# One core, one layer step with Mamba-2 and sparse attention: seven re-orderings in a hand-scheduled kernel (attention units in one visit, tanh of the convolution apart from its taps, a third weight buffer, bias tables by matmul, quads in the state update)

## The chip, the cores and the metric

The kernel runs on one core of one Trainium2 chip, as one launch. The metric is the device time of one execution in microseconds (us). The kernel before was timed three times: 1399.72, 1389.86 and 1389.57 us, median 1389.86. The profile is of one execution of its own, which took 1398.44 us.

## The reference

One inference step of a decoder layer for two request groups that share the weights: a prompt of 256 tokens, and 8 samples of 8 new tokens each over 2048 cached positions. Together they are 320 columns of activations.

```python
def layer_forward(x, ssm_state, conv_state, nsa_fn, bias_tab, lw):
    x = x + 0.5 * swiglu_ffn(rmsnorm(x, ffn1_norm), ffn1_w_in, ffn1_w_out)
    h = rmsnorm(x, mix_norm)
    z, xbc, dt_raw, q, kv, nsa_g, merge_g = jnp.split(h @ w_in_proj, cuts, axis=-1)
    y_ssm, new_conv, new_ssm = mamba_mixer(z, xbc, dt_raw, conv_state, ssm_state, ...)
    q = rmsnorm(q.reshape(b, L, KV_HEADS, Q_PER_KV, HEAD_DIM), qk_norm[0]) * (HEAD_DIM ** -0.5)
    ...
    gates = jax.nn.sigmoid(nsa_g.astype(f32)).reshape(b, L, KV_HEADS, Q_PER_KV, 3)
    o, new_win = nsa_fn(q, gates, paged_rows, win_rows, compress_kv, bias_tab)
    gm = jax.nn.sigmoid(merge_g.astype(f32))
    y_a = (y_ssm @ w_branch_ssm).astype(f32)
    y_b = (o.reshape(b, L, D_ATTN).astype(x.dtype) @ w_branch_attn).astype(f32)
    mix = (gm[..., :D_MODEL] * y_a + gm[..., D_MODEL:] * y_b).astype(x.dtype) @ w_out
    x = x + mix
    x = x + 0.5 * swiglu_ffn(rmsnorm(x, ffn2_norm), ffn2_w_in, ffn2_w_out)

def causal_conv(xbc, conv_state, w, b):          # in mamba_mixer, before the state update
    ...
    y = b + sum(xp[:, k:k + L] * w[k] for k in range(D_CONV))
    return jax.nn.silu(y), xp[:, L:]

def ssd(x, dt, A, Bm, Cm, h0):                   # in mamba_mixer: chunked scan
    ...
    states = jnp.einsum('bclgn,bclgjp->bcgjpn', Bc, xdt * decay_to_end[..., None])
    ...
    y_off = jnp.einsum('bclgn,bcgjpn->bclgjp', Cc, h_start) * decay_from_start[..., None]

def nsa_block(...):                              # nsa_fn, per block of queries
    ...                                          # three softmaxes with a relative bias on each score:
    return gates[..., 0:1] * o_c + gates[..., 1:2] * o_s + gates[..., 2:3] * o_w
```

The three branches of the attention are compressed keys (`o_c`), the best blocks of keys (`o_s`) and a window (`o_w`).

## The kernel before

**Dense work.** Every large product goes through `dense` (L327). Weights are split in two fp32r halves, as are the activations, so a step over 128 rows of weights (a k-step) is three matmuls of 128x128 by 320 columns: L342, L343 and L344. The kernel has 1928 k-steps, in this order: FFN1, the projection of q, k and v, that of the convolution's channels (xBC), the merge gates, z, the two branch products and `w_out`, FFN2.

**Weights.** They come in blocks of 8 k-steps (128x1024) through the queue of SP (`w_load`, L305) into one of `NRAW` = 2 raw buffers. ACT casts a block to its high half `wh` (L314), DVE subtracts to the low half `wl` (L323), and only then the next load is issued. Cast and subtraction run two blocks ahead of the matmuls.

**Order.** Each engine works through its instructions in the order in which the program issues them. That order is written by generators: after each k-step `tick` (L143) adds half of the stage's number in `RATE` (L116) to a credit, and for each whole credit one generator goes on to its next `yield`. What the generators put on PE in one such step lies between two k-steps and is called a visit here. `S.defer(n, f)` runs f after 2n k-steps. So attention, compression of the cache and the state update lie between the dense matmuls, and a wait of any of them on PE holds up everything behind it.

**The places of the change.**

- Convolution (`conv_unit`, L1199): one unit per 128 channels; 4 k-steps after its projection three taps on DVE, directly followed by the tanh on ACT; the gate on DVE 8 k-steps after the projection.
- Attention: 32 units of the prompt (xBC stage) and 40 of the samples (z stage), 8 batches of 5. A unit has a visit with the transposes of the next unit (L1302, L1457) and scores (L1431) further ahead, then a `yield`, then a visit with its own values (L1319, L1471). ACT copies transposed weights to `pT` or `sT`. At each batch edge of the samples ACT copies the sums to `R` (L1477).
- Bias tables `tb` and `cb`: each of their 128 rows is a shifted row of a reversed table that lies in DRAM (`trev`): 16 strided DMAs on SP (`load_bias`, L837). `flip`, a constant, is loaded by SP just before them (L849).
- State update of the samples (`sample_chunks`, four groups q of 8 batches): states `h` come 4 ahead (`AHEAD`) into 6 buffers (`NH`), on SP (L1726). For two batches at a time PE does two output products from the states (L1772, 32 columns of the array) and for each of them two products of the update (L1778 with 128 rows, L1779 with the low half, 64 rows). POOL decays h (L1775), DVE adds (L1780), SP stores it (L1679).

```python
                    if b % 2 == 0:
                        for x_ in range(2):
                            r = 32 * ((b + x_) % 4)
                            pe.matmul(py[r : r + 32, :], cz[:, b + x_, :], pend["h", j + x_], start=b + x_ < 4,
                                      stop=b + x_ >= 4)
                    ...
                    pe.matmul(p, bz[:, b, :], xh, start=True, stop=False)
                    pe.matmul(p, bz[:64, b, :], xl, start=False, stop=True)
                    v.tensor_tensor(h0, h0, p, op=ALU.add)
                    store("outH")
                    pend["outH"] = O["ssmS"][b, :, 512 * q : 512 * q + 512], h0
                    load_h(j + AHEAD)
```

## Time and profile before

| | |
|---|---|
| three runs, median | 1399.72, 1389.86, 1389.57 us: 1389.86 us |
| profiled execution | 1398.44 us, span of the trace 1396.4 us |
| granted TensorE clock, mean of the span | 0.961 |
| busy: PE (matmuls), PEld (weight loads) | 1329.4 us (95%), 1177.7 us (84%) |
| busy: DVE, ACT, POOL | 866.0, 592.8, 363.5 us (62%, 42%, 26%) |
| moved by DMA | 251.66 MB, 180 GB/s in the mean |

The span is the trace from the first to the last instruction; a share is busy time over it. Busy PE contains matmuls that run at half the clock, and matmuls that wait for their weights, so 95% isn't 95% of what PE can do. The granted clock is given as a share of 2.4 GHz: 1.00 is 2.4 GHz all through, 0.5 is 1.2 GHz all through, and a value between them says how the stretch divides between the two levels.

### The profile page before, as it was taken

To read this page: it belongs to the slowest core of one execution; us is meant where nothing else is said; L and a number is where in the kernel's file an instruction comes from. 1 tells how busy PE (TensorE), PEld (TensorE's weight loads), DVE (VectorE), ACT (ScalarE), POOL (GpSimd) and SP (SyncE) were. 2 spreads that over 40 slices of the span, in tenths; PEclk is the share of its full clock that TensorE was granted. 3 is DMA by queue.
4 is the path that set the end of the run, shared out by engine and by line. 5 is a ranking of instruction groups with operands and counts; after the bars stand their busy time and mean duration, and the time that the engine had idled before them with its cause. 6 is when DMAs were issued, how large, how long until landed. Compare 5 with 4: busy or idle time off the path is not lost.

```text
span 1396.4 us, 28186 instructions
## 1 busy us (share of the span) xinstructions
PE 1329.4 (95%) x10583; PEld 1177.7 (84%) x10583; DVE 866.0 (62%) x1862; ACT 592.8 (42%) x1152; POOL 363.5 (26%) x616
## 2 busy tenths in 40 slices
PE   8999999999979999889989989799999999999998
PEld 7899999999858878677877756577677999999998
DVE  5577656655556457866567657657767766666533
ACT  4454543445434324446544343255555344333322
POOL 2222212222000216554444435233340010000000
PEclk9999999999989999889999999999999999999999
DMA  7556656666544325421177686778894443444453
GB/s 258 164 192 201 221 184 198 210 205 201 209 100 126 125 96 198 182 91 61 50 197 214 190 237 181 290 249 314 267 333 148 168 140 134 149 149 151 148 171 110
DMA packets 107041, 251.66 MB, mean 180 GB/s; under 512 B 23208, under 2 KB 49849, under 8 KB 104953
## 3 DMA queue, kind: packets, MB, share of 16 engines
q1 hardware_dynamic: 89946, 198.27, 44.2%
q0 software_dynamic: 16960, 51.61, 11.1%
q8 instruction: 83, 1.36, 0.4%
q14 instruction: 52, 0.43, 0.1%
HBM read 235.11 MB, written 23.10 MB: 185 GB/s over the span
## 4 chain that ended last, share of the span: by engine, by line
PE 72%; DVE 11%; DMA 5%; issue 4%; ACT 4%; SPq 2%; POOL 1%; POOLq 0%; ACTq 0%; DVEq 0%
PE ps_pd L342 18%; PE ps_pd L343 16%; PE ps_pd L344 16%; DVE wl L323 3%; PE ps_sc L671 2%; PE ps_sc L672 2%; PE ps_sc L681 2%; ACT wh L314 2%; PE ps_sc L1431 2%; DVE cvo L1198 2%; PE ps_po L1471 1%; DMA out_ssmS<-h 1%; PE ps_pt L1457 1%; PE ps_po L1319 1%; PE ps_sc L1270 1%
## 5 line engine op out<-in xcount | busy, mean ns | idle before, releaser
L323 DVE TENSOR_TENSOR wl<-wraw,wh 128x1024 fp32r<-128x1024 f32 (+1 forms) x245 | 302.0, 1233 | 266.9 <-ACT wh L314 266.4
L342 PE MATMUL ps_pd<-hh,wh 128*128 128x320 f32 x1320 | 452.5, 343 | 4.5 <-ACT hh L751 1.8
L343 PE MATMUL ps_pd<-hl,wh 128*128 128x320 f32 x1320 | 418.0, 317 | 1.6 <-DVE hl L450 1.4
L344 PE MATMUL ps_pd<-hh,wl 128*128 128x320 f32 x1320 | 417.2, 316 | 0.0
L314 ACT CAST wh<-wraw 128x1024 fp32r<-128x1024 f32 (+1 forms) x245 | 252.7, 1031 | 167.2 <-PE ps_pd L343 125.0
L342 PEld LDWEIGHTS ps_pd<-hh,wh 128*128 128x128 f32 x1320 | 257.4, 195 | 44.6 <-issue 32.8
L343 PEld LDWEIGHTS ps_pd<-hl,wh 128*128 128x128 f32 x1320 | 257.6, 195 | 10.2 <-issue 5.3
L344 PEld LDWEIGHTS ps_pd<-hh,wl 128*128 128x128 f32 x1320 | 256.5, 194 | 0.0
L342 PE MATMUL ps_pd<-ah,wh 128*128 128x320 f32 x352 | 109.4, 311 | 0.0
L344 PE MATMUL ps_pd<-ah,wl 128*128 128x320 f32 x352 | 108.7, 309 | 0.0
L343 PE MATMUL ps_pd<-al,wh 128*128 128x320 f32 x320 | 98.7, 309 | 0.0
L563 POOL DMA_DIRECT2D pg<-in_cache x136 | 74.3, 547 | 73.6 <-DVE pgl L575 30.6
L235 POOL TENSOR_SCALAR ah<-ff 128x320 fp32r<-128x320 f32 x44 | 20.1, 458 | 277.9 <-DVE ff L478 277.8
L575 DVE TENSOR_TENSOR pgl<-pg,pgh 128x512 fp32r<-128x512 f32 x128 | 82.4, 685 | 15.1 <-ACT pgh L568 14.9
L1384 POOL DMA_DIRECT2D KV<-in_cache x102 | 55.0, 539 | 104.3 <-PE ps_po L1471 68.5
L473 ACT ACTIVATE sg<-sg 128x320 f32<-128x320 f32 x44 | 20.8, 472 | 135.1 <-DVE sg L472 135.0
L568 ACT CAST pgh<-pg 128x512 fp32r<-128x512 f32 x128 | 72.6, 616 | 9.0 <-PE ps_sc L672 7.3
L671 PE MATMUL ps_sc<-pgh,w1h 128*128 128x256 f32 x256 | 68.6, 289 | 2.5 <-ACT pgh L568 2.5
L672 PE MATMUL ps_sc<-pgh,w1l 128*128 128x256 f32 x256 | 68.6, 288 | 0.0
L342 PEld LDWEIGHTS ps_pd<-ah,wh 128*128 128x128 f32 x352 | 66.1, 188 | 0.5
L344 PEld LDWEIGHTS ps_pd<-ah,wl 128*128 128x128 f32 x352 | 66.1, 188 | 0.0
L343 PEld LDWEIGHTS ps_pd<-al,wh 128*128 128x128 f32 x320 | 60.2, 188 | 0.0
(453 smaller groups left out, 2250.2 us busy)
## 6 DMA issues: line engine op xcount, KB each, us to landing
wraw<-in_wproj SPq DMA_DIRECT2D x77, 512.0 KB
KV<-in_cache POOLq DMA_DIRECT2D x102, 256.0 KB, 5.4
wraw<-in_w1in SPq DMA_DIRECT2D x44, 512.0 KB
wraw<-in_w2in SPq DMA_DIRECT2D x44, 512.0 KB
pg<-in_cache POOLq DMA_DIRECT2D x136, 128.0 KB, 4.1
pg<-in_cache SPq DMA_DIRECT2D x120, 128.0 KB
wraw<-in_w1out SPq DMA_DIRECT2D x16, 512.0 KB
h<-in_ssm SPq DMA_DIRECT2D x32, 256.0 KB
```

The costliest lines, as they stand in the source:

```text
L314: a.copy(h[:, :n], st["raw"][i][:, :n])
L323: v.tensor_tensor(l[:, :n], st["raw"].pop(i)[:, :n], st["hl"][i][0][:, :n], op=ALU.subtract)
L342: pe.matmul(out, wh[:, s], xh[:, kk, :], start=kk == 0, stop=False)
L343: pe.matmul(out, wh[:, s], xl[:, kk, :], start=False, stop=False)
L344: pe.matmul(out, wl[:, s], xh[:, kk, :], start=False, stop=kk == K - 1)
L563: e.dma_start(page(s, half)[:, i, :], I["cache"][ds(r, 1), :, 256 * c : 256 * c + 256].rearrange("o p f -> p (o f)"))
L568: a.copy(h[:, 8 * half : 8 * half + 8, :], page(s, half)[:, :, 64 * q : 64 * q + 64])
L575: v.tensor_tensor(l[:, 8 * half : 8 * half + 8, :], page(s, half)[:, :, 64 * q : 64 * q + 64], h[:, 8 * half : 8 * half + 8, :], op=ALU.su ...
L671: pe.matmul(ph, wh[:, j, :], h[:, :, j, :], start=q + j == 0, stop=False)
L672: pe.matmul(ph, wl[:, j, :], h[:, :, j, :], start=False, stop=False)
L681: pe.matmul(ph, wh[:, j, :], l[:, :, j, :], start=False, stop=q + j == 6)
L1384: e.dma_start(t[:, j, :], I["cache"][ds(r, 1), :, 512:1024].rearrange("o p f -> p (o f)"))
```

## The change

Seven things at once. The tanh of a convolution unit is issued 3 k-steps after its taps, and the gate 11 instead of 8 k-steps after the projection; `defer` keeps its list in order of time. Each attention unit is one visit: the `yield` ahead of `values` is gone, and the numbers in `RATE` are lower for the stages (xBC, z, branch products) that held two visits per unit. There are three raw weight buffers, with one load more at the start, and `wl` is made after the third k-step of a block, not the second. `tb` and `cb` are computed by 24 matmuls (48 instructions) in the FFN1 stage, instead of 16 strided DMAs; `flip` is loaded there too. The first transposes of the compressed keys come 3 steps later. In the state update, four output products stand together, `xl` has 128 rows, `NH` is 8 and `AHEAD` 5, a load of h stands ahead of the store, and the first group waits 6 steps more. The sums of squares of `w_out` come 4 k-steps later, and the DMA scratch is smaller.

```diff
-W0, W1, W2, W3, WS, EB = 3, 3, 6, 1, 8, 2
+W0, W1, W2, W3, WS, EB = 3, 3, 6, 1, 4, 2
...
-RATE = (0.59, 1.2, 0.9, 1.5, 0.85, 1.0, 1.0)
+RATE = (0.59, 1.2, 0.9, 1.1, 0.88, 0.54, 1.0)
...
     def defer(self, n, f):
-        self.later.append([n, f])
+        i = len(self.later)
+        while i and self.later[i - 1][0] > n:
+            i -= 1
+        self.later.insert(i, [n, f])
...
-    NRAW, SA = 2, 2
+    NRAW, SA = 3, 2
...
-                if k == 1:
+                if k == 2:
                     w_lo()
...
-        if i == 1:
+        if i % 2:
             w_load()
...
+    tb, cb, flip = kcv[:, 2048:2056], kcv[:, 2056:2120], kcv[:, 2120:2248]
...
+        gcopy(relz[:, 7::8][:, 0:16], rel[:, 0:16])
+
+        p = bank("sc", (128, 72))
+        last = lambda t: oht[:, 6 - t : 7 - t] if t < 7 else oh[:, 2047:2048]
+        for o, n, src in ((0, 8, lambda t: oht[:, 7 - t : 15 - t]), (8, 63, lambda t: oh[:, 38 - t : 2048 - t : 32][:, 0:63]),
+                          (71, 1, last)):
+            for t in range(T):
+                pe.matmul(p[:, o : o + n], relz[:, 7 - t : 135 - t], src(t), start=t == 0, stop=t == T - 1)
+        a.copy(kcv[:, 2048:2120], p)
         release("oh")
+        sp.dma_start(flip, I["con"][:, C_KEEP : C_KEEP + 128])
...
-        yield from wait(4)
+        yield from wait(7)
         for q in range(2):
...
-        flip = st["blob"][:, 4600:4728]
-        sp.dma_start(flip, I["con"][:, C_KEEP : C_KEEP + 128])
-        load_bias(tb, PAST, 8)
-        load_bias(cb, 31, 64, 32)
...
             for k in range(1, 4):
                 v.scalar_tensor_tensor(o, pr[:, k : k + 344], w(k), o, op0=ALU.mult, op1=ALU.add)
+
+        def tanh():
             a.activation(th, o, AF.Tanh)
...
         S.defer(2, taps)
-        S.defer(4, gate)
+        S.defer(3.5, tanh)
+        S.defer(5.5, gate)
...
             if i + 4 < 32:
                 scores(i + 4)
-            yield
             values(i)
...
             if groups and groups[0][0] <= i + 3:
                 scores(*groups.pop(0))
-            yield
             if i and i % 5 == 0:
...
-        NH, AHEAD = 6, 4
+        NH, AHEAD = 8, 5
...
-            xl = sx.tile([64, 512], F32R, tag="xl", bufs=1, name="xl")
+            xl = sx.tile([128, 512], F32R, tag="xl", bufs=1, name="xl")
...
-            pend["lo"] = xl, xde[:64], xh[:64]
+            pend["lo"] = xl, xde, xh
...
+                if q == 0:
+                    yield from wait(6)
                 stage_b(q, 2)
...
-                    if b % 2 == 0:
-                        for x_ in range(2):
-                            r = 32 * ((b + x_) % 4)
-                            pe.matmul(py[r : r + 32, :], cz[:, b + x_, :], pend["h", j + x_], start=b + x_ < 4,
-                                      stop=b + x_ >= 4)
+                    if b % 4 == 0:
+                        for x_ in range(4):
+                            r = 32 * x_
+                            pe.matmul(py[r : r + 32, :], cz[:, b + x_, :], pend["h", j + x_], start=b == 0, stop=b == 4)
...
-                    pe.matmul(p, bz[:64, b, :], xl, start=False, stop=True)
+                    pe.matmul(p, bz[:, b, :], xl, start=False, stop=True)
                     v.tensor_tensor(h0, h0, p, op=ALU.add)
+                    load_h(j + AHEAD)
                     store("outH")
                     pend["outH"] = O["ssmS"][b, :, 512 * q : 512 * q + 512], h0
-                    load_h(j + AHEAD)
...
-    sq = Squares(8, 3)
+    sq = Squares(8, 5)
```

The names in the lists below are those of the program with the numbers of their buffers' uses: `ps_` are PSUM tiles, `h0_` and a number is one state, `wraw` a raw weight block. Line numbers behind the change are those of its own code.

On PE, in the state update of the samples, before (group q=1, its first two batches):

```order
L1772 MATMUL ps_po_8835<-h0_8549,cz_8133 32x512
L1772 MATMUL ps_po_8835<-h0_8557,cz_8133 32x512
L1778 MATMUL ps_sc_8839<-xh_8759,bz_8763 128x512
L1779 MATMUL ps_sc_8839<-xl_8760,bz_8763 128x512
L1778 MATMUL ps_sc_8847<-xh_8759,bz_8763 128x512
L1779 MATMUL ps_sc_8847<-xl_8760,bz_8763 128x512
L342 MATMUL ps_pd_8829<-hh_4690,wh_8680 128x320
```

and the same place now:

```order
L1783 MATMUL ps_po_8996<-h0_8640,cz_8101 32x512
L1783 MATMUL ps_po_8996<-h0_8676,cz_8101 32x512
L1783 MATMUL ps_po_8996<-h0_8684,cz_8101 32x512
L1783 MATMUL ps_po_8996<-h0_8728,cz_8101 32x512
L1788 MATMUL ps_sc_9002<-xh_8883,bz_8887 128x512
L1789 MATMUL ps_sc_9002<-xl_8884,bz_8887 128x512
L1788 MATMUL ps_sc_9010<-xh_8883,bz_8887 128x512
L1789 MATMUL ps_sc_9010<-xl_8884,bz_8887 128x512
L345 MATMUL ps_pd_8943<-hh_4720,wh_8758 128x320
```

The four output products need four states at once, and the visit of the next two batches has none.

On SP, the queue of weights and states in the same group, before (`out_ssmS` is a store of a state, `h0<-in_ssm` a load):

```order
L1679 DMA out_ssmP<-St_8570 128x512
L1679 DMA out_ssmS<-h0_8495 128x512
L1726 DMA h0_8844<-in_ssm 128x512
L1679 DMA out_ssmS<-h0_8549 128x512
L1726 DMA h0_8852<-in_ssm 128x512
L305 DMA wraw_8859<-in_wproj 128x1024
L1679 DMA out_ssmS<-h0_8557 128x512
L1726 DMA h0_8872<-in_ssm 128x512
L1679 DMA out_ssmS<-h0_8591 128x512
```

and now:

```order
L308 DMA wraw_8865<-in_wproj 128x1024
L1402 DMA bias_8898<-trev_79 16x2x512 x16
L1404 DMA wb_8915<-in_wm 128x8
L1589 DMA abs_8939<-ascr_80 64x8x64
L1589 DMA ab_8981<-ascr_80 128x8x128
L308 DMA wraw_8988<-in_wproj 128x1024
L1734 DMA h0_9006<-in_ssm 128x512
L1687 DMA out_ssmS<-h0_8632 128x512
L1734 DMA h0_9014<-in_ssm 128x512
L1687 DMA out_ssmS<-h0_8640 128x512
L1734 DMA h0_9028<-in_ssm 128x512
```

The loads of the states for the second four products of the group now stand behind the 16 bias DMAs of the sample attention, and `h0_9028` goes into the buffer that `h0_8632` is stored from, three entries ahead of it.

On ACT, in the xBC stage with the prompt attention, before (`cvt` is a tanh, `qn` takes the sums of eight units, `pT` transposed weights of attention, `pS` their exponentials):

```order
L1303 COPY pT_6917<-ps_pt_6916 128x256
L1279 ACTIVATE pS_6923,pm_6924<-pS_6923,pm_6924 128x128 x2
L1199 ACTIVATE cvt_6904<-cvo_6903 128x344
L1323 COPY qn_4810<-ps_po_6491 128x8x64
L1303 COPY pT_6963<-ps_pt_6962 128x256
L1279 ACTIVATE pS_6969,pm_6970<-pS_6969,pm_6970 128x128 x2
L1187 COPY pr0_4835<-ps_pd_6907 128x256
```

and now:

```order
L1313 COPY pT_6862<-ps_pt_6861 128x256
L1289 ACTIVATE pS_6868,pm_6869<-pS_6868,pm_6869 128x128 x2
L1333 COPY qn_4840<-ps_po_6501 128x8x64
L1313 COPY pT_6903<-ps_pt_6902 128x256
L1289 ACTIVATE pS_6909,pm_6910<-pS_6909,pm_6910 128x128 x2
L1208 ACTIVATE cvt_6849<-cvo_6848 128x344
L1313 COPY pT_6939<-ps_pt_6938 128x256
L1289 ACTIVATE pS_6945,pm_6946<-pS_6945,pm_6946 128x128 x2
```

The tanh (L1199, now L1208) stood directly ahead of the copies that PE's next visits need (L1323 and L1303, now L1333 and L1313), and now stands behind them.

## Rows read from the trace of the kernel before

**Rows 1.** The page: busy time, share of the span and instructions of each engine; and the chain of work that ended last, its shares by engine.

```profile
PE 1329.4 (95%) x10583; PEld 1177.7 (84%) x10583; DVE 866.0 (62%) x1862; ACT 592.8 (42%) x1152; POOL 363.5 (26%) x616
...
PE 72%; DVE 11%; DMA 5%; issue 4%; ACT 4%; SPq 2%; POOL 1%; POOLq 0%; ACTq 0%; DVEq 0%
```

**Rows 2.** Waits of PE over the whole span: what the waiting instruction writes and its line, what it waited for and that line, then us in total, times, the longest in us.

```profile
PE ps_sc L1431 <- DVE ms L1444: 6.0, 1, 6.0
PE ps_pt L1637 <- POOL abs L1627: 5.4, 1, 5.4
PE ps_pt L392 <- ACT sq L365: 5.1, 4, 1.8
PE ps_sc L855 <- DMA blob<-in_con: 4.4, 1, 4.4
PE ps_sc L1778 <- ACT btok L1608: 4.4, 1, 4.4
PE ps_po L1319 <- ACT qn L1323: 4.1, 1, 4.1
PE ps_pt L1302 <- ACT blob L1264: 3.6, 2, 2.6
...
PE ps_sc L733 <- DVE kcv L727: 2.5, 1, 2.5
PE ps_po L1471 <- ACT R L1477: 2.3, 2, 1.2
PE ps_po L1319 <- ACT pT L1303: 2.2, 2, 2.0
...
PE ps_po L1772 <- DMA h<-in_ssm: 0.3, 1, 0.3
```

**Rows 3.** Stretches of the span around the longest of these waits: the stretch and its length in us, busy time of PE, PEld, DVE, ACT and POOL (instructions), the mean granted clock, the DMA share and GB/s.

```profile
404.00:420.00 16.00, 11.56 (x45) 7.19 (x44) 2.45 (x2) 3.89 (x7) 0.00 (x0) 0.79 0.62 73
574.00:612.00 38.00, 28.43 (x194) 24.67 (x193) 29.06 (x82) 16.43 (x54) 18.00 (x39) 0.78 0.41 152
709.00:726.00 17.00, 11.58 (x73) 10.72 (x74) 9.90 (x21) 8.92 (x20) 6.88 (x5) 0.80 0.50 153
...
800.00:816.00 16.00, 11.58 (x49) 6.06 (x49) 5.77 (x10) 2.27 (x4) 6.21 (x5) 0.79 0.86 240
...
894.00:914.00 20.00, 14.03 (x108) 9.01 (x108) 7.77 (x19) 7.49 (x15) 4.86 (x9) 0.74 0.84 330
```

**Rows 4.** Timeline of PE's matmuls in the state update: start in us, duration in us, engine, line, what it writes and reads, tile and shape. From start to start is the pitch.

```profile
767.22 0.30 PE L343 MATMUL ps_pd<-hl,wh 128*128 128x320 f32 x1
767.36 0.31 PE L344 MATMUL ps_pd<-hh,wl 128*128 128x320 f32 x1
767.60 1.05 PE L1772 MATMUL ps_po<-h,cz 128*32 128x512 f32 x4
768.58 0.50 PE L1778 MATMUL ps_sc<-xh,bz 128*128 128x512 f32 x1
769.01 0.50 PE L1779 MATMUL ps_sc<-xl,bz 64*128 64x512 f32 x1
...
770.31 0.42 PE L342 MATMUL ps_pd<-hh,wh 128*128 128x320 f32 x1
```

**Rows 5.** Timeline of PE's weight loads in the same place, same columns.

```profile
769.01 0.18 PEld L1779 LDWEIGHTS ps_sc<-xl,bz 64*128 64x128 f32 x1 [0.25 <-issue]
...
770.42 0.19 PEld L343 LDWEIGHTS ps_pd<-hl,wh 128*128 128x128 f32 x1
```

**Rows 6.** Timeline of PE at 55 us, 32 matmuls of one column, same columns.

```profile
55.47 4.87 PE L602 MATMUL ps_po<-par,pg 128*128 128x1 f32 x32
```

**Rows 7.** The chain that ended last, in order of time, at 829 us: start in us, us, what (a 128x128 f32 matmul of 128 columns).

```profile
829.80 0.11 PE ps_sc L1603
```

**Rows 8.** Waits of ACT from 540 to 700 us, columns as in rows 2.

```profile
ACT cvt L1199 <- DVE pm L1287: 25.4, 7, 4.9
ACT cvt L1199 <- DVE cvo L1198: 23.5, 10, 3.5
```

**Rows 9.** Timeline of ACT at 604 us; the bracket is the idle time before an instruction, in us, and what ended it.

```profile
604.64 0.49 ACT L1199 ACTIVATE cvt<-cvo 128x344 f32<-128x344 f32 x1 [4.48 <-DVE pm L1287]
```

**Rows 10.** Waits of SP's queue from 700 to 890 us, columns as in rows 2.

```profile
SPq L1726 <- DMA out_ssmS<-h: 43.0, 15, 6.1
SPq L305 <- DVE wl L323: 41.3, 11, 6.5
```

**Rows 11.** Timeline of SP's queue at 789 us, and of ACT at 804 and at 898 us (bracket as in rows 9).

```profile
789.60 10.51 SPq L1393 DMA_DIRECT2D bias<-trev  x16
...
804.18 1.04 ACT L314 CAST wh<-wraw 128x1024 fp32r<-128x1024 f32 x1 [5.44 <-DMA wraw<-in_wproj]
...
898.71 1.04 ACT L314 CAST wh<-wraw 128x1024 fp32r<-128x1024 f32 x1 [5.90 <-DMA wraw<-in_wproj]
```

**Rows 12.** The chain that ended last, in order of time, at 814 us, columns as in rows 7.

```profile
814.36 4.88 DMA out_ssmS<-h
...
819.25 5.57 DMA h<-in_ssm
```

**Rows 13.** Timeline of ACT in the sample attention at a batch edge.

```profile
1020.19 0.72 ACT L1450 ACTIVATE P<-P,ms 128x512 f32<-128x512 f32 x1
...
1021.22 1.05 ACT L314 CAST wh<-wraw 128x1024 fp32r<-128x1024 f32 x1
```

More of the change, by code (lines that the diff above doesn't have):

```diff
@@ L524, in step_kernel @@
     pew = cp.tile([128, 2], F32, name="pew")
-    rel = fp.tile([NBK + 1, 32], F32, name="rel")
     held, LAG, numbers = [], 1, {}
@@ L621, in cmp_stream @@
         yield
+        oht = fp.tile([NBK + 1, TL - 2048 + 168], F32, tag="hid", bufs=1, name="oht")
+        rel = oht[:, TL - 2048 : TL - 2016]
+        relz = oht[:, TL - 2016 :]
+        g.memset(relz, 0.0)
         g.memset(rel, -BIG)
@@ L637, in cmp_stream @@
             p = bank("sc", (32, NT))
-            pe.matmul(p[:, :n], rel, oh[:, k : k + n] if k < 2048 else oht, start=True, stop=True)
+            pe.matmul(p[:, :n], rel, oh[:, k : k + n] if k < 2048 else oht[:, 0 : TL - 2048], start=True, stop=True)
             tv = tp.tile([32, NT], F32, tag="sq", name="tv")
@@ L814, in step_kernel @@
     pq = q0.enter_context(tc.tile_pool(name="pq", bufs=1))
-    tb = pq.tile([128, 8], F32, name="tb")
-    cb = pq.tile([128, 64], F32, name="cb")
     vst = pq.tile([128, 256], F32, name="vst")
@@ L827, in bl, with load_bias @@
         return st["blob"][:, o : o + m * n].rearrange("p (a b) -> p a b", a=m)
-    for c in range(2):
-        sp.dma_start(w1b[:, c], I["w1c"][:, c])
     tr0 = trev[0:16, :]
-    def load_bias(dst, k0, n, step=1):
+    def load_bias(dst, k0, n):
         for t in range(T):
-            src = bass.AP(tensor=tr0.tensor, offset=tr0.offset + 7 - t + k0, ap=[[TL, 16], [step, n]])
+            src = bass.AP(tensor=tr0.tensor, offset=tr0.offset + 7 - t + k0, ap=[[TL, 16], [1, n]])
             sp.dma_start(dst[t :: T, :], src)
@@ L1327, in prompt_attn @@
         build(0)
-        yield from wait(2)
+        yield
         cmp_a(0)
-        yield from wait(4)
+        yield from wait(3)
         cmp_b(0, 0)
@@ L1849, in done @@
         yield IDLE
-    early = chain(cmp_keys(), prompt_bias(), selector(), until("gates"), both(gates_rows(), decays()))
+    bias_ = prompt_bias()
+    next(bias_)
+    for c in range(2):
+        sp.dma_start(w1b[:, c], I["w1c"][:, c])
+    early = chain(cmp_keys(), bias_, selector(), until("gates"), both(gates_rows(), decays()))
     S.rate = RATE[1]
```

8 lines of the change are left out of this document (4 added, 4 removed).

## The prediction

> **What bounds the kernel.** I read the page first [rows 1]: PE is busy in 95% of the span and holds 72% of the chain of waits; no other engine is over 62%. So a wait counts if PE stands in it. The list of PE's waits [rows 2] shows where: single waits of 2 to 6 us, each at one place, for POOL, DVE, ACT or a DMA, and hardly one that repeats. Then the table of stretches [rows 3]: in the 16 to 38 us around such waits the granted clock is 0.74 to 0.80 in the mean. With the two levels 2.4 and 1.2 GHz, 0.79 over 16 us means that 6.7 us ran at 1.2 GHz (1 - 2 x 0.21 = 0.58 of it at full speed). Dense matmuls do half as much there, so a stretch of 6.7 us costs some 3.4 us on top of the wait that it follows. This makes each long wait worth almost twice its length, and these waits are what most of the change touches. The second kind of cost is pitch [rows 4]: two dense matmuls start 0.14 us apart, but the products of the state update 0.43.
>
> The sum is made against the profiled execution, 1398.44 us; the median of the runs is 0.9939 of it (1389.86), and I scale the result by that. A comparison of this kernel can tell about 1% from no change.
>
> **Bias tables on PE: +8.** 48 small f32 instructions in the FFN1 stage. A 128-column f32 matmul took 0.11 us [rows 7], so 5.3. The nearest matmuls with next to no columns took 4.87 / 32 = 0.15 [rows 6], so 7.3 above; below, 0.11 x 48 with half the columns cannot go under some 3. A fall of the clock behind them would add up to 3.4. I take 5.3 and most of that: +8, bounds +3 to +11. What goes away is 16 DMAs ahead of the xBC stage on SP. Their landing is not waited for, but `flip` is: PE stood 4.4 us for it (L855) [rows 2], with 404 to 420 at 0.79 behind it. Loaded in the FFN1 stage it is long there: 4.4 + 3.4, less 0.6 for what PE may wait there instead: **-7.2**, bounds 0 to -8.
>
> **Compressed keys: -3.4.** PE waited 2.5 us for DVE's keys (L733) [rows 2]. The transposes now come five k-steps later, which at 0.44 us each (three pitches of rows 4) are 2.2 us; with part of a clock fall behind it I take -3.4, bounds 0 to -4.
>
> **Tanh: -13.** ACT waited 25.4 and 23.5 us for the taps of a tanh that DVE had not done [rows 8], and everything behind it on ACT waited too; the longest wait before 605 us ended with the tanh at 604.64 [rows 9], and the next thing on ACT was the copy `qn` that PE stood 4.1 us for. With the waits for the copies `blob` (2.6) and `pT` (2.0), which stood behind a tanh likewise, that is 8.7 us; 574 to 612 at 0.78 means 16.7 us at 1.2 GHz, so 8.4 more. Of these 17.1 I leave 4 for waits that stay, since DVE is no faster and the gate, which DVE does later now, is also waited for. The tanh is 3 k-steps later (1.3 us) and behind the copies in ACT's order. Bounds 0 to -17.
>
> **One visit per unit: -2.** Dense to other work and back costs about 0.1 us each way: L344 starts at 767.36 and the visit at 767.60, which is 0.1 more than the pitch of 0.14. But a unit's transposes, scores and values have different shapes; of its switches only one back and forth with the dense steps goes, and only where scores of a 32-column shape stand ahead of values of the same. I count 24 units at 0.1: -2. Were each of the 72 units to save 0.2, it would be -14; 0 is the other end. The work itself is unchanged.
>
> **State update.** Four terms, and one against.
> - The `xl` product with 128 rows. The pair L1778 and L1779 alternates between a 128-row and a 64-row tile, and each starts 0.43 us after the one before [rows 4], with its weight load starting only then [rows 5]. In dense steps a weight load runs while the matmul before it streams (L343's load at 770.42 beside the matmul from 770.31). With equal shapes I put a 512-column product at 0.23, from the dense pitch per column (0.14 x 512 / 320). That is 4 products x 0.2 + 0.15 for the switch = 0.95 in each of 16 visits: **-15**, bounds 0 to -16.
> - Four output products together: two take 0.98 us (767.60 to 768.58), four go to different columns of the array and cost what two do. Eight pairs fewer: 8 x 0.98 = **-8**, bounds 0 to -8.
> - The first group waits for 6 more steps. PE stood 5.4 us for POOL's `abs` (L1637), and 709 to 726 was at 0.80 (3.4 more); 8.8 less a rest: **-8**.
> - At 802 us PE stood 4.4 us for `btok` (L1778), which ACT did late because its cast before waited 5.44 us for a weight block [rows 11]; that block was issued behind the 16 bias DMAs on SP, which take 10.51 us to issue [rows 11]. With a third raw buffer the block is issued before them. With 800 to 816 at 0.79: 7.8 less a rest, **-7**.
> - Against it: the states. The wait of L1772 for a load is now 0.3 us in all [rows 2]. In the new order four states must have landed at once, or PE stands with all dense steps behind it, and a load goes into a buffer whose store stands just ahead of it in SP's queue (the SP list of the change). SP's loads already wait for stores, 43.0 us in 15 waits [rows 10], and on the chain a store took 4.88 us and the load behind it 5.57 [rows 12]: 10.5 us from store to state. From one quad to the next PE has two visits and their dense steps, some 7 us. So 3.3 us are short in q2 and q3. In q1 the 16 bias DMAs stand ahead of the loads: 10.51 us of issue, less a cover of 2: 8.5. In q0, with 8 buffers still fresh, 1.5. Sum 16.6, with one clock fall: **+20**, bounds +5 (only q1's issue) to +58 (8 quads that each wait 7.2).
>
> **Sample attention at 896 us: -9.** PE stood 6.0 us for DVE's `ms` (L1431), which came late because ACT's cast waited 5.90 us for its block [rows 11], and DVE's subtraction with it. 894 to 914 at 0.74 is 10.4 us at 1.2 GHz, 5.2 lost. 11.2 less 2, since `KV` loads stand around that block: -9, bounds 0 to -11. The third raw buffer does this too: SP's load waits for `wl` 41.3 us [rows 10], and now has one buffer more.
>
> **Copy of the sums at a batch edge: +5.** Values of the next batch wait for ACT's copy `R`: 2.3 us in 2 waits now [rows 2]. With one visit per unit, scores, copy and values stand closer by one gap of two k-steps (0.9 us), and the copy stands behind an exponential (0.72) or a cast (1.05) [rows 13]. 7 edges x 0.7 = +5, bounds +1 to +12.
>
> **Sums of squares behind `w_out`: -2.5.** A quarter of the 5.1 us of L392 [rows 2], plus a clock fall of half a stretch. At nothing I cost the subtraction to `wl` one k-step later (it runs two blocks, 16 k-steps, ahead of its matmul; without that lead it would cost 0.44 a block), the gate (a whole group of six units lies between it and its reader) and the smaller scratch.
>
> **Sum.** 8 - 7.2 - 3.4 - 13 - 2 - 15 - 8 - 8 - 7 + 20 - 9 + 5 - 2.5 = -42. 1398.44 - 42 = 1356, times 0.9939: **1348 us**, own range 1334 to 1362.
>
> **Rivals.**
> - *Bigger gain*: PE waits neither for states nor for `R`, as now (0.3 us for states) [rows 2]. 42 + 25 = 67: 1331, scaled 1323. For it: 8 buffers and loads issued ahead of stores. Against it: rows 10 and 12.
> - *The third buffer does not bring loads forward.* SP's queue is in order; where a load of a state waits for a store ahead of a block's load, the free buffer is not filled. Then the terms at 709, 800 and half of that at 896 come back, 20 us: 1376, scaled 1368.
> - *No drain gain.* If a weight load runs beside a matmul only where the rows of the array differ, 128-row pairs are no faster than now; -15 falls away: 1371, scaled 1363. The dense steps speak against it: loads of 128 rows at 770.42, beside a 128-row matmul [rows 5]. The rule is that of the Trainium skill, TensorE: Matmul & The Clock Gate, "What overlaps and what doesn't": weight loads overlap with matmuls in flight only when their row group differs. By it the sum would be 1363, by the row 1348; the trace of this kernel disagrees with it.
> - *No change*: each of the eight quads waits for the whole store and load behind it, 10.5 less 3.3 of cover: 58 instead of 20, so -42 + 38: 1394, scaled 1386.
> - *Slower*: the 40 sample units. Values follow the transposes of the next unit directly and need `sT` of their own, copied by ACT since the last visit, 3.7 k-steps (1.6 us) earlier at the new rate. If ACT has an exponential (0.72) and a cast (1.05) ahead of it then [rows 13], and nothing of the 1.6 us is left but 0.4, the copy comes 1.8 - 0.4 = 1.4 us late in each unit: +56. -42 + 56: 1412, scaled 1404. It decides from the point at which ACT's queue is over 1.6 us deep at a visit; ACT is busy 42% of the span [rows 1], which speaks against it.
>
> **Chances.** Forecast 0.51, bigger gain 0.15, third buffer without effect 0.12, no drain gain 0.06, no change 0.09, slower 0.07. The range takes in all but the last two: 1318 to 1382. Faster by over 1% (under 1376): 0.83; within 1%: 0.10; slower by over 1%: 0.07.
>
> **What would show it.** After the change the list of PE's waits has no L855, L1637 or L1778 lines of 4 us; L1788 and L1789 start about 0.23 us apart; four L1783 together take about 1 us; the state products wait for `h<-in_ssm` for some 17 us in all, most of it in q1; ACT's tanh waits are shorter than 25 us. I am wrong if the prompt attention still has waits of 2 to 4 us (then the tanh was not the late one), or if new waits of PE for `sT` or `h` exceed 40 us.

## The result: half a per cent, and the profile after

The changed kernel took 1387.39 us (median of 20 runs), the kernel before 1396.11 us (20 runs): a ratio of 0.9947, 95% interval 0.9921 to 0.9972. It is faster, by 0.5% where 3% was predicted, and 1387 us lies above the range of 1318 to 1382. The profiled execution took 1394.21 us, its span is 1392.6 us at a mean granted clock of 0.959 (before 1396.4 at 0.961).

The page after, busy times, to be held against [rows 1]:

```profile
PE 1318.9 (95%) x10631; PEld 1183.5 (85%) x10631; DVE 868.7 (62%) x1862; ACT 592.6 (43%) x1155; POOL 361.9 (26%) x618
```

PE's waits after (columns as in rows 2). Of the waits that the change went for, those for `in_con`, `btok` and the keys are gone; `ms` is down from 6.0 to 1.4 us, `abs` from 5.4 to 0.7 (with 2.7 for `ab` beside it), the squares (`sq`) from 5.1 to 2.7 and `qn` from 4.1 to 2.1 [rows 2]. Others stand in their place:

```profile
PE ps_po L1480 <- ACT R L1486: 12.2, 6, 4.6
PE ps_po L1783 <- DMA h<-in_ssm: 6.3, 5, 3.5
PE ps_sc L644 <- DMA pg<-in_oh: 4.9, 1, 4.9
PE ps_pt L1251 <- POOL blob L1244: 4.3, 2, 3.4
PE ps_sc L1788 <- DVE h L1790: 4.1, 8, 1.2
PE ps_sc L1046 <- issue: 3.8, 1, 3.8
PE ps_pt L395 <- ACT sq L368: 2.7, 2, 1.7
PE ps_pt L1645 <- POOL ab L1635: 2.7, 1, 2.7
PE ps_pd L347 <- DVE wl L326: 2.5, 3, 0.9
PE ps_pt L1312 <- POOL pS L1300: 2.3, 2, 2.0
PE ps_po L1329 <- ACT qn L1333: 2.1, 1, 2.1
...
PE ps_pd L345 <- ACT hh L261: 1.8, 1, 1.8
```

The stretches around the new waits (columns as in rows 3):

```profile
27.00:46.00 19.00, 13.55 (x51) 9.00 (x51) 6.19 (x10) 5.47 (x9) 2.52 (x5) 0.73 0.59 173
55.00:71.00 16.00, 15.76 (x98) 15.48 (x97) 5.28 (x8) 5.11 (x10) 1.91 (x4) 0.79 0.22 70
404.00:420.00 16.00, 15.19 (x95) 12.99 (x94) 11.13 (x21) 6.79 (x13) 0.22 (x2) 1.00 0.48 153
556.00:593.00 37.00, 28.50 (x343) 26.02 (x343) 22.70 (x76) 15.80 (x56) 13.99 (x40) 0.83 0.49 181
...
787.00:805.00 18.00, 13.53 (x51) 7.50 (x50) 7.75 (x10) 2.10 (x5) 7.02 (x7) 0.81 0.86 279
896.00:916.00 20.00, 19.99 (x248) 15.35 (x251) 12.27 (x46) 11.23 (x26) 6.45 (x12) 1.00 0.93 332
946.00:960.00 14.00, 10.49 (x118) 8.64 (x126) 7.79 (x34) 5.01 (x13) 4.30 (x8) 0.76 0.59 200
1148.00:1164.00 16.00, 14.06 (x66) 13.55 (x65) 8.55 (x23) 5.18 (x8) 0.88 (x1) 0.68 0.39 129
```

404 to 420 and 896 to 916 are at 1.00 now (0.79 and 0.74 around there before [rows 3]), but 27 to 46, 55 to 71, 946 to 960 and 1148 to 1164 stand at 0.68 to 0.79. The stages of the prompt attention and of the state update still have such a stretch each, 556 to 593 and 787 to 805 at 0.83 and 0.81, where 574 to 612 and 800 to 816 had 0.78 and 0.79 [rows 3]. The mean clock of the span is no better. That is the result in one sentence: long waits were taken out and others came in, and the granted clock falls around the new ones as it did around the old.

Since the dense work is the same in both, the start of the n-th k-step can be read in both traces, and the time between two k-steps compared (us, one profiled execution each):

| k-steps | what runs there | before | after | change | predicted |
|---|---|---|---|---|---|
| 0-75 | start, bias tables | 57.7 | 73.2 | +15.5 | +8 |
| 75-525 | compression of the cache | 305.9 | 303.5 | -2.4 | 0 |
| 525-575 | keys, prompt biases | 53.3 | 43.5 | -9.9 | -10.6 |
| 575-725 | q, k, v; compressed keys of the prompt | 105.8 | 107.8 | +2.0 | 0 |
| 725-875 | convolution, prompt attention | 164.7 | 170.2 | +5.5 | -13 |
| 875-1060 | state update | 187.8 | 179.5 | -8.3 | -18 |
| 1060-1235 | sample attention | 194.0 | 187.0 | -7.0 | -6 |
| 1235-1375 | branch products | 66.4 | 62.9 | -3.5 | 0 |
| 1375-1425 | `w_out` | 27.3 | 31.6 | +4.3 | -2.5 |

(The -2 for one visit per unit stands with the samples.) In the runs below a stretch whose code is unchanged can move by some 5 us (575 to 725 takes 103 to 108 us), and 20 to 50 even by 10, so less is read only where it is the same in every run. The -3.5 is (62.9 to 63.1 us in each, 64.0 with the attention part alone), but no run shows what it comes from.

### The profile page after: what moved, and what is told of

It reads as the page before. It is cut to its first block, busy times and chain, and to the rows that moved or that the text cites. A ratio compares the mean times of both kernels' runs of the same rounds, so it can differ in the third digit from the quotient of the medians.

```text
span 1392.6 us, 28257 instructions
## 1 busy us (share of the span) xinstructions
PE 1318.9 (95%) x10631; PEld 1183.5 (85%) x10631; DVE 868.7 (62%) x1862; ACT 592.6 (43%) x1155; POOL 361.9 (26%) x618
## 5 line engine op out<-in xcount | busy, mean ns | idle before, releaser
L345 PE MATMUL ps_pd<-hh,wh 128*128 128x320 f32 x1320 | 443.5, 336 | 6.2 <-ACT hh L767 2.1
L578 DVE TENSOR_TENSOR pgl<-pg,pgh 128x512 fp32r<-128x512 f32 x128 | 82.4, 685 | 30.4 <-ACT pgh L571 29.9
```

The costliest lines, as they stand in the source:

```text
L345: pe.matmul(out, wh[:, s], xh[:, kk, :], start=kk == 0, stop=False)
L578: v.tensor_tensor(l[:, 8 * half : 8 * half + 8, :], page(s, half)[:, :, 64 * q : 64 * q + 64], h[:, 8 * half : 8 * half + 8, :], op=ALU.su ...
```

## The experiments

Each is the changed kernel with one edit, unless it says otherwise. Ratios are to the kernel before, timed beside it; the changed kernel's own is 0.9947.

### Bias tables on PE

```diff
-        gcopy(relz[:, 7::8][:, 0:16], rel[:, 0:16])
...
-                pe.matmul(p[:, o : o + n], relz[:, 7 - t : 135 - t], src(t), start=t == 0, stop=t == T - 1)
-        a.copy(kcv[:, 2048:2120], p)
...
+        load_bias(tb, PAST, 8)
+        load_bias(cb, 31, 64, 32)
```

> The changed kernel with the 24 bias matmuls taken out again and tb and cb loaded by the 16 strided DMAs on SP, now behind the prompt's bias loads; flip stays loaded early. Theory A (the matmuls cost PE 7.5 us and a fall of the clock, and the DMAs are not waited for): the stretch from k-step 50 to 75 goes back from 28 to 19 us, the stretch from 525 to 575 stays within 2 us of 43.5, so about 9 us faster than the changed kernel, ratio to before 0.988. Theory B (the DMAs held up SP's queue before, flip and weights behind them): 525 to 575 gets 5 to 8 us longer again and the ratio stays at 0.993 to 0.996. If the fall of the clock before k-step 50 comes from the reordered loads at the start alone, 20 to 50 stays 7 to 9 us longer than before.

Measured: 1375.39 us, ratio 0.9857 (0.9810 to 0.9904). K-steps 50 to 75 take 17.3 us (27.9 with the matmuls, 18.9 before), 525 to 575 take 44.4 (43.5). Theory A. The matmuls cost PE (timeline of the changed kernel's PE):

```profile
56.58 1.95 PE L656 MATMUL ps_sc<-oht 33*128 33x8 f32 x16 [0.24 <-POOL oht L238]
58.39 2.01 PE L656 MATMUL ps_sc<-pg,oht 33*128 33x63 f32 x16
60.22 3.05 PE L656 MATMUL ps_sc<-oht 33*128 33x1 f32 x14
63.14 0.56 PE L656 MATMUL ps_sc<-pg,oht 33*128 33x1 f32 x2
```

From 56.58 to the next dense matmul at 63.63 are 7 us for 48 instructions. The clock parts them (columns as in rows 3; the third row is the same 48 in `prompt_two`, a run below, where the clock falls later):

```profile
56.58:60.22 3.64, 3.64 (x32) 3.64 (x33) 0.00 (x0) 0.00 (x0) 0.00 (x0) 1.00 0.51 165
60.22:63.63 3.41, 3.41 (x19) 3.40 (x18) 0.00 (x0) 0.00 (x0) 1.15 (x2) 0.50 0.37 115
56.76:62.37 5.61, 5.61 (x50) 5.59 (x49) 0.00 (x0) 0.00 (x0) 1.13 (x2) 0.96 0.40 130
```

At 2.4 GHz they start 0.11 us apart, the price that the prediction took [rows 7], and at 1.2 GHz 0.21. The 0.15 of [rows 6] is a mean of the two levels as well: there the granted clock is 1.00 from 55.47 to 57.60 us and 0.50 behind it. So the price of an instruction was right, and what stands above it is the clock, which falls while the matmuls run and is at 0.79 in the mean of 55 to 71 us. The DMAs that they replaced cost 0.9 us at most (525 to 575) once `flip` no longer stands behind them.

K-steps 20 to 50 stay 8 us longer than before here too (29.9 us, 21.9 before), so that part of the loss is not the matmuls. Nor is it shown to be the change: kernels with the same start differ (21.8 us in `pairs`, 21.7 in `lo_k1_sq3`, 20.9 in `taps1`, 29.6 in `nraw2`), and `visits_only`, whose start is that of the kernel before, takes 26.1. The short ones stand at a granted clock of 1.00 there. Those of 26 us and more stand at 0.76 to 0.83, each with a wait of PE of 1.6 to 4.9 us, mostly for a load of the bias tables' inputs that came late (`in_oh`, L644 above), in `nraw2` and `visits_only` for DVE's `sg`.

### Convolution and prompt attention

```diff
-        def tanh():
             a.activation(th, o, AF.Tanh)
...
-        S.defer(3.5, tanh)
-        S.defer(5.5, gate)
+        S.defer(4, gate)
```

> The changed kernel with the tanh directly behind the taps again and the gate 8 k-steps behind the projection; all else as changed. Theory A (the tanh's place is worth what I predicted, 13 us, and something else in the xBC stage ate it): 13 us slower than the changed kernel, ratio to the kernel before about 1.004, and ACT's waits in that stage for the taps (cvt <- DVE) back at some 50 us. Theory B (DVE's chain of the softmax sets the pace there; the tanh only handed its wait on to the exponentials behind it): within 4 us of the changed kernel, ratio 0.992 to 0.998, ACT's waits moved from the exponentials (40.5 us now) back to the tanh, their sum unchanged at about 60 us.

Measured: 1387.00 us, ratio 0.9946 (0.9924 to 0.9969): no difference. Theory B. ACT's waits in this stage (530 to 710 us, columns as in rows 2), with the tanh later and then with it back:

```profile
ACT pS L1289 <- DVE pm L1286: 40.5, 21, 6.7
...
ACT cvt L1208 <- DVE cvo L1205: 11.6, 3, 4.6
```

```profile
ACT cvt L1206 <- DVE pm L1294: 27.4, 8, 7.4
ACT cvt L1206 <- DVE cvo L1205: 26.4, 10, 4.5
ACT pS L1286 <- DVE pm L1283: 10.8, 13, 2.4
```

The tanh's waits are 11.6 us after the change and 53.8 with it back, and the exponentials wait instead: 52 us against 65 in all, every one for DVE. PE's time from 725 to 875 is 166.1 us with the tanh back, 170.2 as changed. To see whether DVE sets the pace, two taps of three were left out (the convolution is not computed):

```diff
-            for k in range(1, 4):
+            for k in range(1, 2):
```

> The changed kernel with two of the three taps of each convolution unit left out on DVE, some 1.2 us in each of 24 units; it does not compute the convolution. Theory A (DVE's queue is what the prompt attention waits for, so every order of the same work gives the same time): the stretch from k-step 725 to 875, 170.2 us now and 164.7 before, gets 10 to 20 us shorter, and the waits of PE for pm, blob, pS and qn there, 15 us, fall to under 5. Theory B (it is the distance of the steps, and DVE has room): within 4 us.

Measured: 1369.11 us, ratio 0.9830 (0.9782 to 0.9878); 725 to 875 in 152.8 us, 17.4 less than as changed. The stretch as changed, then here (columns as in rows 3):

```profile
536.29:706.47 170.18, 152.09 (x1514) 129.36 (x1513) 114.26 (x346) 85.73 (x260) 83.46 (x176) 0.93 0.32 115
528.53:681.35 152.82, 143.69 (x1515) 122.08 (x1513) 91.55 (x310) 86.92 (x263) 83.11 (x179) 0.99 0.37 127
```

Theory A in the size: with 22.7 us less of DVE the stretch is 17.4 us shorter and the clock rises from 0.93 to 0.99, so DVE's work there is on PE's path. Of the waits that the expectation names, 13.5 us in this stretch as changed, 8.7 are left, not under 5, so DVE is not all that PE waits for. A version that keeps the work and moves a tap to POOL, on top of `bias_dma`:

```diff
+        g.tensor_scalar(o1, pr[:, 1:345], w(1), None, op0=ALU.mult)
+        g.tensor_tensor(o, o, o1, op=ALU.add)
...
-            for k in range(1, 4):
+            for k in range(2, 4):
```

> Bias tables by DMA, and one of the three taps of each convolution unit moved from DVE to POOL (two instructions there, which is busy in 84 of the 170 us of that stage). Theory A (DVE's queue paces the prompt attention): k-step 725 to 875 gets 6 to 10 us shorter than the 170 us of the changed kernel, and the ratio to before 0.978 to 0.982. Theory B (the taps come later through POOL, which waits for its own turns, or POOL and DVE slow each other): no gain or a loss, ratio 0.985 or above.

Measured: 1392.97 us, ratio 0.9977 (0.9943 to 1.0012); 725 to 875 in 184.2 us (168.2 in `bias_dma`), with PE's waits for POOL's `blob` at 8.4 us (4.3). Theory B: the two instructions on POOL cost more than the tap on DVE saves. POOL is busy 133.6 us of the stretch (83.0 in `bias_dma`), DVE 109.8 (114.3).

### One visit or two

Two visits for the prompt, then for the samples, then the attention part of the change alone on the kernel before:

```diff
             if i + 4 < 32:
                 scores(i + 4)
+            yield
             values(i)
...
-RATE = (0.59, 1.2, 0.9, 1.1, 0.88, 0.54, 1.0)
+RATE = (0.59, 1.2, 0.9, 1.5, 0.88, 0.54, 1.0)
...
-        yield
+        yield from wait(2)
         cmp_a(0)
-        yield from wait(3)
+        yield from wait(4)
```

> The changed kernel with two visits per unit of the prompt attention again (the yield ahead of values, rate 1.5, the start waits 2 and 4 steps). Theory A (one visit per unit costs here: the stage from k-step 725 to 875 came out 5.5 us longer where 15 shorter was predicted): 12 to 18 us faster than the changed kernel, ratio to before about 0.984. Theory B (the stage is paced by DVE, whatever the visits are): within 4 us, ratio 0.992 to 0.998.

```diff
                 scores(*groups.pop(0))
+            yield
             if i and i % 5 == 0:
...
-RATE = (0.59, 1.2, 0.9, 1.1, 0.88, 0.54, 1.0)
+RATE = (0.59, 1.2, 0.9, 1.1, 0.88, 1.0, 1.0)
```

> The changed kernel with two visits per unit of the sample attention again (yield ahead of values, rate 1.0 from there). Theory A (the merged visit makes PE wait for ACT's copy R: 12.2 us in 6 waits, with the clock falling behind the longest): 8 to 14 us faster, ratio about 0.988, waits for R at 2 to 3 us. Theory B (the waits are ACT's and DVE's depth at the batch edge and come back under another name): within 4 us.

> The kernel before with the attention part of the change alone: one visit per unit for prompt and samples, the rates, the start waits and WS as in the changed kernel. Theory A (fewer, larger visits make no work less, and their longer stalls bring TensorE's clock down; the two-visit runs had mean clocks of 0.964 to 0.969 against 0.9615): 4 to 10 us slower than before, ratio 1.003 to 1.007, mean clock 0.957 or less. Theory B (neutral by itself, the gain of two visits needs the other parts): 0.998 to 1.002.

Measured: prompt in two visits 1382.44 us, 0.9917 (0.9880 to 0.9953); samples in two visits 1386.78 us, 0.9930 (0.9904 to 0.9956), with 6.4 us of waits for `R` where 2 to 3 were expected, neither apart from 0.9947; the part alone 1402.36 us, 1.0067 (1.0051 to 1.0083): slower. Theory A has the size but not the cause: the mean clock of that kernel's runs is 0.961, against 0.964 of the kernel before beside it. The stretches tell more. In their own stretch the visits are neutral (725 to 875: 163.4 us with the part alone, 164.7 before; 1060 to 1235: 195.6 and 194.0). What moves is the stage behind: 875 to 1060 takes 195.8 us with the part alone (187.8 before), and 171.8 with the prompt in two visits (179.5 as changed), 8 us each way. With the part alone all of it lies at the beginning: 875 to 920 takes 46.7 us (36.7 before). The last values of the prompt stand at k-step 862 with one visit per unit and at 871 with two, and the state update starts as much earlier: its first product with POOL's `abs` or `ab` stands at k-step 898 in the part alone, 907 before, 911 as changed, 919 with two visits. PE's wait there, in the part alone and, as changed, in the list above (2.7 us; 5.4 before [rows 2]; none over 1 us with two visits):

```profile
PE ps_po L1470 <- ACT R L1476: 12.0, 7, 4.7
PE ps_pt L1635 <- POOL abs L1625: 8.6, 1, 8.6
```

So an attention that ends nine k-steps earlier meets inputs that are not there yet. Both edits undone on `bias_dma`:

> Bias tables by DMA (the run before: 1.4% faster than before) and two visits per attention unit in the prompt's and the samples' stages, with their former rates 1.5 and 1.0. If one visit per unit is neutral, as the two single runs had it (both within 5 us of the changed kernel): ratio 0.982 to 0.989, the same as with the bias tables by DMA alone. If the visits cost each a little that the single runs hid: 0.975 to 0.981.

Measured: 1368.95 us, ratio 0.9787 (0.9733 to 0.9841), against 0.9857 with one visit. That is the size of the second expectation, but the two intervals overlap. PE's waits for `R` are 3.4 us there, and 12.0 to 15.3 in the runs with one visit per sample unit. The timeline of ACT shows one of them, as changed:

```profile
943.43 0.72 ACT L1459 ACTIVATE P<-P,ms 128x512 f32<-128x512 f32 x1
...
944.47 1.03 ACT L317 CAST wh<-wraw 128x1024 fp32r<-128x1024 f32 x1
948.68 0.47 ACT L368 ACTIVATE sqa<-xbc 128x320 f32<-128x320 f32 x1 [3.18 <-DVE xbc L1958]
949.05 0.41 ACT L1486 COPY R<-ps_po 128x320 f32<-128x320 f32 x1
```

The copy `R` at 949.05 stands behind a square of the z stage (`sqa`, L368) that itself waited 3.18 us for DVE; PE stood 4.65 us for it.

### Third raw buffer, and the subtraction

```diff
-    NRAW, SA = 3, 2
+    NRAW, SA = 2, 2
...
-        if i % 2:
+        if i == 1:
```

> The changed kernel with two raw weight buffers and without the additional load at the start. The third buffer helped where PE waited at 802 and 896 us before (13.8 us from k-step 1075 to 1100, some 8 around 987), and cost some 7.6 at the start, where PE now waits 4.9 us for pg<-in_oh. Theory A: both are true, so 8 to 14 us slower than the changed kernel (ratio about 1.003), with the wait for in_oh gone. Theory B (those two stalls went by the moved bias DMAs and the reordered queue, not by the buffer): 5 to 8 us faster, ratio about 0.990.

Measured: 1390.06 us, ratio 0.9981 (0.9949 to 1.0014), 2.7 us above the changed kernel and not apart from it. Neither theory in full: with two buffers the stretch 985 to 1010 is 26.5 us (37.9 before, 26.6 as changed) and 1060 to 1100 is 32.7 (46.8 before, 32.3), so the gain at those two places is not the buffer's. The first went with the 16 bias DMAs, which SP now issues elsewhere; of the second only so much is known that it goes with the lower rate (with two visits at the rate 1.0 that stretch is 44.5 us, and 1100 to 1235 as much shorter, so the rate only moves time within the stage).

```diff
-                if k == 2:
+                if k == 1:
...
-    sq = Squares(8, 5)
+    sq = Squares(8, 3)
```

> The changed kernel with the subtraction to wl after the second k-step of a block and the sums of squares of w_out 6 k-steps behind, both as before. Theory A (these two cost what the stretch from k-step 1375 to 1425 lost, 4.3 us, with three waits of PE for wl, 2.5 us): 5 to 8 us faster, ratio 0.990, no waits for wl. Theory B (chance of the clock there): within 3 us.

Measured: 1397.42 us, ratio 1.0025 (0.9996 to 1.0054), 10 us slower than as changed. A miss for both theories: 1375 to 1425 takes 30.0 us (31.6), but so it does in eight kernels that keep both edits, so that is not theirs; 725 to 875 takes 176.7 (170.2), 875 to 1060 183.1 (179.5), 1060 to 1235 190.6 (187.0). Priced at nothing in the prediction, the later subtraction (or the squares, which this run does not part from it; but they lie only in `w_out`) is worth some 10 us. That it gains them because DVE is late in those three stages is argued from the other runs and not shown.

### State update

```diff
-            xl = sx.tile([128, 512], F32R, tag="xl", bufs=1, name="xl")
+            xl = sx.tile([64, 512], F32R, tag="xl", bufs=1, name="xl")
```

> The changed kernel with the low half xl of the state update on 64 rows again. The products then alternate in shape and start 0.43 us apart instead of 0.23, 0.95 us in each of 16 visits. Theory A (PE's time in these visits is on the path): the stretch from k-step 875 to 1060 gets 12 to 16 us longer and the kernel as much slower, ratio to before about 1.004. Theory B (POOL's decay, 1.1 to 1.4 us for each state, and DVE's addition set the pace of the visits, and PE waited for DVE's h 4.1 us in 8 waits): half of it or less, up to 7 us, with the waits for h L1790 gone.

Measured: 1389.70 us, ratio 0.9939 (0.9907 to 0.9971); 875 to 1060 in 184.5 us, 5 more, which is no more than stretches move by themselves, and the time no different. Theory B in time, though the waits for h are not gone (2.8 us in 2, 4.1 in 8 as changed). The pitch itself is as predicted; the timeline of PE as changed (columns as in rows 4):

```profile
743.34 1.06 PE L1783 MATMUL ps_po<-h,cz 128*32 128x512 f32 x8
...
744.67 0.40 PE L1789 MATMUL ps_sc<-xl,bz 128*128 128x512 f32 x1
744.90 0.39 PE L1788 MATMUL ps_sc<-xh,bz 128*128 128x512 f32 x1
...
747.63 0.50 PE L1788 MATMUL ps_sc<-xh,bz 128*128 128x512 f32 x1 [1.23 <-DVE h L1790]
...
748.67 0.50 PE L1788 MATMUL ps_sc<-xh,bz 128*128 128x512 f32 x1 [0.31 <-DVE h L1790]
```

The weight load of the second pair, and DVE in the same place:

```profile
744.91 0.19 PEld L1789 LDWEIGHTS ps_sc<-xl,bz 128*128 128x128 f32 x1
...
745.06 1.91 DVE L326 TENSOR_TENSOR wl<-wraw,wh 128x1024 fp32r<-128x1024 f32 x1
746.90 0.67 DVE L1790 TENSOR_TENSOR h<-h,ps_sc 128x512 f32<-128x512 f32 x1
747.92 0.69 DVE L1790 TENSOR_TENSOR h<-h,ps_sc 128x512 f32<-128x512 f32 x1 [0.35 <-POOL h L1785]
```

Products start 0.23 us apart (0.43 before [rows 4]), with the load at 744.91 beside the matmul from 744.90, and eight instructions of four output products take the 1.0 us that two took. But the next visit, at 747.63, stands 1.23 us for DVE's addition, and its second product again: DVE had a subtraction to `wl` of 1.9 us ahead of the first addition, and the second waited for POOL's decay. What PE saves there it waits.

```diff
-                    if b % 4 == 0:
-                        for x_ in range(4):
+                    if b % 2 == 0:
+                        for x_ in range(2):
```

> The changed kernel with two output products at a time again, all else as changed (8 state buffers, 5 ahead, xl on 128 rows). Theory A (four at once save 8 x 0.98 us on PE, and cost the wait of 12.3 us at k-step 971, since four states must be there): wait for h<-in_ssm under 2 us, 875 to 1060 within 5 us of now, kernel within 5 us of the changed kernel. Theory B (the loads behind the 16 bias DMAs are late for pairs too): 6 to 10 us slower, with the wait as long as now.

Measured: 1391.25 us, ratio 0.9950 (0.9910 to 0.9991), 875 to 1060 in 179.7 us (179.5): quads bring nothing and cost nothing. The wait for states is 3.7 us in 2 with pairs (under 2 was expected), 6.3 in 5 with quads. The longest one as changed, in SP's queue and on PE:

```profile
773.52 10.93 SPq L1402 DMA_DIRECT2D bias<-trev  x16
...
787.13 0.42 SPq L1734 DMA_DIRECT2D h<-in_ssm  x1
...
793.07 1.05 PE L1783 MATMUL ps_po<-h,cz 128*32 128x512 f32 x2 [3.55 <-DMA h<-in_ssm]
```

The loads for the second quad of q=1 are issued behind the 16 bias DMAs. The visit, at k-step 971, takes 12.3 us where such a visit without a wait takes 2.1.

```diff
-W0, W1, W2, W3, WS, EB = 3, 3, 6, 1, 4, 2
+W0, W1, W2, W3, WS, EB = 3, 3, 6, 1, 4, 1
```

> The changed kernel with the 16 bias DMAs of the sample attention issued one prompt chunk earlier, so that they stand ahead of four loads of states earlier and no longer right ahead of those for the second quad of q=1. Theory A (they are what PE waited for at k-step 971, 4.5 us and a stretch at low clock, 12.3 us in all): that visit falls to 3 us and the kernel gets 6 to 9 us faster, ratio 0.989. Theory B (it is the chain store, then load, in the buffers): the wait for h<-in_ssm stays at 5 to 7 us, perhaps at another quad, and the time within 4 us.

Measured: 1390.79 us, ratio 0.9972 (0.9937 to 1.0007). Neither in full: the time is that of Theory B, but the wait for states falls. PE's waits, and DVE ahead of the second of them:

```profile
PE ps_sc L1788 <- DVE h L1790: 7.5, 6, 3.3
PE ps_sc L1788 <- DVE ecb L1654: 4.5, 1, 4.5
...
PE ps_po L1783 <- DMA h<-in_ssm: 3.1, 4, 1.3
...
783.20 1.29 DVE L1600 TENSOR_SCALAR ab<-ab,tk 128x128 f32<-128x128 f32 x2 [6.60 <-DMA ab<-ascr]
```

3.1 us instead of 6.3 for the states, and 4.5 us for `ecb` and 7.5 for h in exchange: SP is at the 16 DMAs for 10.5 us before [rows 11], 10.9 as changed and 11.8 here, and what it issues behind them is late: here `ab`, issued at 775.10 us, for which DVE stands 6.60 us with `ecb` behind it.

> The changed kernel without POOL's decay of the states (L1785 left out, 32 multiplications of 1.1 to 1.4 us), so the states it stores are not the right ones. Theory A (POOL's decay, then DVE's addition, set the pace of the state update, so that 128-row products and quads freed PE for nothing): the waits of PE for DVE's h (4.1 us) go, and the stretch from k-step 875 to 1060, 179.5 us now, gets 8 to 14 us shorter. Theory B (the queue of loads and stores sets it): the wait for h<-in_ssm stays at 5 to 7 us and the stretch within 4 us.

> The changed kernel with 27 of the 32 stores of the samples' states left out (those states do not come out). Theory A (a load waits for the store of the buffer it goes to): the waits of SP for out_ssmS go, those of PE for h<-in_ssm fall from 6.3 to under 2 us, and the stretch from k-step 875 to 1060 gets 6 to 12 us shorter. Theory B (the 16 bias DMAs ahead of the loads are what is late, or POOL and DVE set the pace): it stays within 4 us.

Measured: without the decay 1384.70 us, 0.9940 (0.9917 to 0.9964); without the stores 1383.66 us, 0.9939 (0.9907 to 0.9970). Neither is apart from 0.9947 in time; 875 to 1060 is 172.1 and 172.0 us, some 7.5 shorter in both, as Theory A of the stores and nearly that of the decay had it. Without the decay PE still waits 5.1 us for DVE's h, so POOL is not the one late engine; without the stores one wait of 3.6 us for a state remains, behind the bias DMAs. Both seem to have a part; since the whole time did not move, how much each is worth is not shown.

Last, the fastest of these (`bias_two`) with more states ahead:

```diff
-        NH, AHEAD = 8, 5
+        NH, AHEAD = 10, 7
```

> Bias tables by DMA, two visits per unit, and in the state update 10 buffers with loads 7 ahead. If PE's remaining 6.5 us of waits for h<-in_ssm are a matter of depth: 5 to 8 us faster than with 8 and 5 (0.9787), 0.973 to 0.976. If the loads only wait for stores sooner: the same, 0.977 to 0.981.

Measured: 1359.38 us, ratio 0.9756 (0.9729 to 0.9783), faster than both kernels, the expected direction at the edge of the expected size; 875 to 1060 in 164.1 us (171.5), PE's waits for states 4.6 us in one wait (6.5 in 6). Its interval overlaps with that of `bias_two`, so the gain from depth alone is not shown beyond the stretch.

## Why the prediction was wrong, point by point

The sum was -42 us; the two profiles differ by -3.8 and the medians by -8.7. The step that failed is one and the same in the largest terms: a wait, or PE's own time, was booked as time of the path, although the engine behind it was late as well.

- **Tanh, -13: failed.** Of 17.1 us only 4 were left for waits that stay because DVE is no faster, and that was the wrong step. The rows [rows 8] name DVE as what ACT waited for; taking the tanh out of ACT's way leaves DVE as late as it was. `tanh_back` shows 0, `taps1` shows that the time hangs on DVE's work. The prediction's own sign of being wrong is there: the prompt attention still has waits of 2 to 4 us (`blob` 3.4, `pS` 2.0, `qn` 2.1).
- **State update, -15 and -8 on PE: mechanism right, place wrong.** Pitch and quads came out as worked out, 0.23 and 1.0 us. But I took PE's time in these visits as time of the path, where DVE's addition and SP's loads are late as well: 5 us of 15 at most (`xl64`) and 0 of 8 (`pairs`) arrive. The wait for states that I set against it is there, 6.3 us where some 17 were expected, mostly at one place, the visit at k-step 971.
- **First group of the state update, -8: its size came,** 875 to 920 takes 28.3 us (36.7 before). No run parts the 6 steps from the earlier end of the attention, which costs 10 us there.
- **Bias matmuls, +8: size.** 10.6 by `bias_dma` (17.3 and 27.9 us from 50 to 75). The 0.11 for an instruction holds at 2.4 GHz; the fall of the clock was too small in the sum, since it comes while they run. The other 8 us of the start are not theirs, and not shown to come from the change at all.
- **Third buffer, -7 and -9: the stalls went, but not by the buffer** (`nraw2`). The stall at 802 us, behind the bias DMAs, came back at k-step 971 as the wait for states behind the same DMAs: I booked the first as a gain of the buffer and the second to the quads, and it is one thing that moved.
- **`flip` and keys, -10.6: right,** -9.9, and the same in every run.
- **Copy `R`, +5: right place, too small,** 12.2 us against 2.3, so +10; in the case shown the copy stood behind a square that waited for DVE, not only behind an exponential and a cast. But the sample stretch as a whole came out as predicted, and two visits give the same (186.0).
- **One visit, -2: its effect lies a stage later.** Alone it costs some 9 us (`visits_only`: 1.0067).
- **Subtraction to `wl`, at nothing: some -10** (`lo_k1_sq3`). This is luck of the forecast: with the subtraction and the squares as before, the change is no gain at all (1.0025).
- **Squares, -2.5: +4.3.** PE's wait for the squares in `w_out`, 1.3 us before, is gone, but 1.8 us for ACT's `hh`, which come behind the sums, stand at 1151.96 us instead, and 1148 to 1164 us is at 0.68. `lo_k1_sq3` has the wait for the squares again (2.5 us) and takes 30.0 us there as well, so where the squares stand is not what decides.
- The rivals: none was it alone. The no-change rival came nearest in time (1386), by luck: its chain of store and load, 58 us of waits, is 6.3 us, one of several places where the gain went. *No drain gain* fell with the pitch of 0.23 us: a 128-row weight load runs beside a 128-row matmul. This trace disagrees with the rule of the Trainium skill (TensorE: Matmul & The Clock Gate, "What overlaps and what doesn't"), which lets a load overlap only where the row group differs. The stretches at 1.2 GHz were counted out with each wait apart; the mean clock stayed (0.961, 0.959), since the new waits bring their own.

What stays open: what removed the stall at 896 us and shortened the sample stage, how DVE's, POOL's and SP's lateness share in the state update, why `w_out` takes 30 to 31.6 us with the change and 27.3 before, and what shortened the branch products.

## What to carry to other kernels

A wait is worth its length only if the engine behind it is early for the next thing: ask what the releaser's releaser does next, and take the queue that is last (here DVE in the attention, SP and DVE in the state update) as the price. Before giving PE more to do to spare DMAs, look whether anything waits for those DMAs. When a stage is made to end earlier, look at what the next stage needs first.
